# Scores of the dilated and block-sparse heads on 64 rows each, two heads side by side

## The chip, the cores and the metric

The kernel runs on one core of one Trainium2 chip. The metric is the device time of one execution in microseconds (us). Three executions of the kernel before took 2421.84, 2419.41 and 2421.93 us; their median is 2421.84.

## The reference, cut to what matters

Two transformer blocks on 512 tokens of 1024 features, all in float32. The first mixes tokens with two kinds of heads (latent attention, "MLA", and dilated windows) and has 32 routed experts; the second has softmax heads over blocks ("MoBA"), stick-breaking heads, a gated delta rule and two dense feed-forward layers. The change is in two of these places.

The dilated branch has 3 groups of 8 heads of 64 features. Group 0 looks back 128 tokens; group 1 does so within each of 4 residues of the token number modulo 4, group 2 within each of 16. Per head, tile of 128 queries and its 128 or 256 keys:

```python
s = einsum('bqhd,bkhd->bhqk', q, k) * dh ** -0.5          # 64 features are contracted
s = where(valid, s - slope[h] * delta * stride, -inf)     # a linear bias, and the window
m = max(s); p = exp(s - m); den = sum(p); o = (p / den) @ v
```

The maximum and the denominator of every group are kept, because the three groups are joined in one softmax. The MoBA heads (8, also of 64 features) come to plain causal softmax at 512 tokens: with two blocks of 256 every past block is chosen.

## The kernel before, in words

Scores need the queries and keys with the features on the partitions. Two heads of 64 features share the 128 partitions of a tile. So that one head's score can be made by a matmul over all 128 rows, the queries lie in a tile with twice the room, `dq` [128, 4 pairs, 2 heads, 512] (`mq` for MoBA): for head 0 rows 64 to 127 are zeros, for head 1 rows 0 to 63. `Dilated.q` sets these zeros with two memsets on POOL (L1724, L1725; L583, L584 for MoBA) and its `evict` writes the halves, one with ACT (L1730, L611) and one with VectorE (L1731, L612).

`Dilated.pair` does two heads of a group (four pairs a group, L1752). It works in jobs: in group 0 a job is one query tile for both heads (four jobs), in groups 1 and 2 it is two query tiles for both heads (two jobs). A job has one PSUM bank `dS` of the tag "s". In it, for each of its two or four scores: the score matmul (L1772, float32, which stands in the trace as two passes, each a weight load and a matmul) and behind it a bf16 matmul that adds bias and mask (L1775). Then VectorE takes the maxima (L1777, L1779), ACT makes one exponential per score (L1788), TensorE transposes the blocks (L1795, `dPT`), VectorE copies them (L1799, `pt`), and TensorE multiplies with the values (L1801, `dO`): 64 columns per head, head 0 to PSUM partitions 0 to 63, head 1 to 64 to 127, the two heads' products one after the other in the program.

`causal_pair` (L313 to L340) serves MLA (96 rows per head) and MoBA. For each of four query tiles and each of two heads: a bank, the score over 128 to 512 keys (L321), a bf16 mask matmul (L322), and `softmax_tile`. Then, per key tile, transposes (L330), a copy for head 0 on VectorE (L336) and for head 1 on ACT (L334), and the products with the values (L339, `OM` for MoBA).

The tag "s" has two banks, "t" two, "o" one, "acc" three. What stands in which order on an engine is not the order of the program text: a planner takes each engine's instructions as its own estimate says that their operands and buffers are ready, and among the ready ones that which stands first in the program. So products of later steps (the next group's projection `acc`, the gate products `gps`, the stick-breaking projections `sps`) stand between the steps of attention on TensorE. At run time each engine keeps that order and waits on semaphores.

Of the kernel before, what the change touches and what calls it, by code (L numbers as in the profile page):

```python
# [9 lines left out]
F32 = mybir.dt.float32  # L10
# [3 lines left out]
AF = mybir.ActivationFunctionType  # L14
# [4 lines left out]
EPS = 1e-6  # L19
# [43 lines left out]
class Model:  # L63
# [25 lines left out]
    def unit(self, src, a, b, pool=None):  # L89
        """Loads a weight unit src [128, a, b] (a * b <= 1024); returns its two float32r parts."""  # L90
# [13 lines left out]
    def split(self, hi, lo, src, eng=None):  # L104
        """hi + lo = src, each in float32r."""
# [57 lines left out]
    def feat_start(self, jobs, nk, rhs):  # L163
        """The first feature-major products after a norm: the first 256 tokens of all, then the others."""
# [7 lines left out]
    def rsqrt_mean(self, pool, ss, n, width, name):  # L172
        """(ss / n + EPS) ** -0.5 on [128, width]."""
# [7 lines left out]
    def norm_tile(self, pool, h, src, grow):  # L181
        """h = rms_norm(src) * grow."""
# [42 lines left out]
    def col(self, pool, ap, p, n, name):  # L225
        """[p, n] tile of a vector: element j * p + i at [i, j]."""
# [71 lines left out]
    def softmax_tile(self, pool, S, n, scale, bufs):  # L298
        """exp(scale * (S - max)) / sum of it, on S [128, n] in PSUM."""
# [143 lines left out]
    def vectors(self, *parts):  # L443
        """Vectors over the features as columns."""
# [12 lines left out]
    def later(self):  # L457
        """What the first products don't need: masks, vectors, what the modulation starts from."""
# [13 lines left out]
    def rows_to_col(self, pool, vec, n, name):  # L472
        """[128, n] tile of a vector of n * 128: element j * 128 + i at [i, j]."""
# [9 lines left out]
    def ada(self, n, layers=(0, 1)):  # L483
        """The next n steps of cond @ ada_w."""
# [38 lines left out]
    def ada_norm(self, pool, l, part, t, bufs=2):  # L523
        """The modulated norm of X's token tile t, transposed, to H; its second part is returned."""
# [5 lines left out]
    def add_out(self, pool, w, nk, lhs, gate, after):  # L530
        """X += gate * (lhs^T w); after(pool, t) is what follows on token tile t."""
# [13 lines left out]
    def second_mix(self):  # L545
# [9 lines left out]
        with ExitStack() as ctx:  # L555
# [12 lines left out]
            # rope tables  # L568
# [41 lines left out]
            def q_evict(sl, p):  # L610
                nc.scalar.activation(qT[:64, :, 0, sl], p[:64], AF.Copy, scale=0.125)  # L611
                nc.vector.tensor_scalar(qT[64:, :, 1, sl], p[64:], 0.125, None, op0=OP.mult)  # L612

            roped(0, q_evict)
# [47 lines left out]
            def out_part(o, r, c, t, us, tag):  # L662
                """X += gate * (o^T w_out's half r) of a token tile and half the columns."""
# [32 lines left out]
    def stick_pair(self, ap, sp, q, k, V, p, oB):  # L696
        """Two stick-breaking heads. Of key tile j, the queries from tile j on, on the free axis."""
# [100 lines left out]
    def gdn(self):  # L798
# [10 lines left out]
        with ExitStack() as ctx:  # L809
# [22 lines left out]
            # decay and step sizes, [128 tokens, tile, head]  # L832
# [55 lines left out]
            def conved(f, dst):  # L888
                """dst = silu(causal convolution of the projection's column tile f)."""
# [10 lines left out]
            def with_norms(f0, dst, extra, between=None):  # L900
                """Eight heads; returns ln of 1 / their lengths as rows, and per token."""
# [970 lines left out]
```

## Time and profile before

| | |
|---|---|
| median of three runs | 2421.84 us |
| profiled execution, first to last instruction (its own time as far as the profile shows it) | 2423.2 us |
| TensorE busy, weight loads busy | 96%, 73% of the span |
| VectorE, ACT, POOL busy | 50%, 35%, 18% |
| attention of dilated group 0, 1, 2 | about 234 to 285, 342 to 364, 444 to 475 us |
| attention of the MoBA heads | about 1060 to 1135 us |
| mean granted TensorE clock | 0.988 |

All stretches are in microseconds from the start of the span. A matmul's row in a timeline has its start and the time to its modelled end; matmuls overlap in the pipeline, so what one costs the engine is read from start to start and not from its length.

### The profile page before, as it was taken

The page shows a single profiled execution, that of the slowest core. Times are in us where ns is not written, and L with a number is a line of the kernel's source. Part 1 is how long each engine was busy: PE and PEld are TensorE (multiplying, and loading weights), DVE is VectorE, ACT ScalarE, POOL GpSimd, SP SyncE. Part 2 cuts the span into 40 slices and gives each one's busy share as a digit, 9 for nine tenths or more (in the row PEclk, how much of TensorE's full clock was granted, in tenths as well). Part 3 has the DMA queues.
Part 4 walks back from the last instruction along what each step waited for, and adds up shares of the span by engine and source line. Part 5 has one row for each costly group of instructions (what it writes and reads, how often), then busy time and mean ns, then how long its engine had stood idle before and what let it go on. Part 6 is the DMA issues. An engine that isn't in the chain of part 4 may idle for free.

```text
span 2423.2 us, 29920 instructions
## 1 busy us (share of the span) xinstructions
PE 2331.5 (96%) x11384; PEld 1761.2 (73%) x11384; DVE 1203.3 (50%) x1939; ACT 851.8 (35%) x1542; POOL 425.3 (18%) x502
## 2 busy tenths in 40 slices
PE   6989999999989999899999999999998999999998
PEld 6567899878844443676668888787667888888886
DVE  5664645455534433655347555424578466333322
ACT  5544333433211111444454223213654444322211
POOL 3233112011111110310001111111030141111111
PEclk9999999999989999999999999999999999999999
DMA  4232133445999994432115556523232123333221
GB/s 124 87 105 87 53 96 108 128 115 161 306 327 371 368 367 173 121 105 69 36 39 152 175 183 199 181 90 107 79 92 65 50 66 120 113 89 103 96 89 68
DMA packets 300281, 330.96 MB, mean 137 GB/s; under 512 B 16832, under 2 KB 241280, under 8 KB 299744
## 3 DMA queue, kind: packets, MB, share of 16 engines
q1 hardware_dynamic: 294128, 310.16, 40.9%
q0 software_dynamic: 6000, 18.79, 2.3%
q8 instruction: 92, 1.51, 0.3%
q14 instruction: 61, 0.50, 0.1%
HBM read 322.49 MB, written 6.41 MB: 136 GB/s over the span
## 4 chain that ended last, share of the span: by engine, by line
PE 83%; DVE 6%; ACT 3%; issue 3%; POOL 3%; DMA 2%; DVEq 0%; POOLq 0%; ACTq 0%
PE acc L119 8%; PE acc L120 8%; PE acc L121 8%; PE fps L119 7%; PE fps L120 7%; PE fps L121 6%; PE gps L119 3%; PE gps L121 3%; PE gps L120 3%; PE py L1453 2%; PE cps L1492 1%; PE S L321 1%; PE cps L1493 1%; PE gp L1004 1%; DMA wraw<-in_ada_w_dram 1%
## 5 line engine op out<-in xcount | busy, mean ns | idle before, releaser
L110 ACT ACTIVATE whi<-wraw 128x1024 fp32r<-128x1024 f32 (+3 forms) x295 | 300.2, 1020 | 452.4 <-PE acc L120 197.6
L114 DVE TENSOR_TENSOR wlo<-wraw,whi 128x1024 fp32r<-128x1024 f32 (+3 forms) x251 | 293.8, 1175 | 312.4 <-ACT whi L110 308.1
L120 PE MATMUL fps<-hhi,wlo 128*128 128x512 f32 (+1 forms) x768 | 286.5, 373 | 0.4 <-DVE wlo L114 0.4
L119 PE MATMUL fps<-hhi,whi 128*128 128x512 f32 (+1 forms) x768 | 286.6, 373 | 0.0
L121 PE MATMUL fps<-hlo,whi 128*128 128x512 f32 (+1 forms) x768 | 284.5, 371 | 0.7 <-DVE hlo L114 0.6
L119 PE MATMUL acc<-whi,hhi 128*128 128x512 f32 (+2 forms) x640 | 258.8, 406 | 0.5 <-DVE qx L1561 0.3
L120 PE MATMUL acc<-whi,hlo 128*128 128x512 f32 (+2 forms) x640 | 251.8, 394 | 1.3 <-DVE hlo L114 1.2
L121 PE MATMUL acc<-wlo,hhi 128*128 128x512 f32 (+2 forms) x640 | 250.8, 393 | 0.0
L114 POOL TENSOR_TENSOR wlo<-wraw,whi 128x1024 fp32r<-128x1024 f32 x44 | 108.2, 2460 | 570.4 <-ACT whi L110 555.8
L495 DVE SCALAR_TENSOR_TENSOR adaacc<-wraw,cond,adaacc 128x1024 f32<-128x1024 f32 x84 | 116.8, 1390 | 107.6 <-DMA wraw<-in_ada_w_dram 107.3
L119 PE MATMUL gps<-hhi,whi 128*128 128x512 f32 (+1 forms) x408 | 158.3, 388 | 6.5 <-DVE gy L895 4.4
L119 PEld LDWEIGHTS fps<-hhi,whi 128*128 128x128 f32 x768 | 144.4, 188 | 27.6 <-issue 0.9
L121 PEld LDWEIGHTS fps<-hlo,whi 128*128 128x128 f32 x768 | 144.3, 188 | 27.3 <-DVE hlo L114 1.1
L120 PEld LDWEIGHTS fps<-hhi,wlo 128*128 128x128 f32 x768 | 144.6, 188 | 24.9 <-DVE wlo L114 0.6
L120 PEld LDWEIGHTS acc<-whi,hlo 128*128 128x128 f32 x640 | 146.0, 228 | 16.6 <-DVE hlo L114 2.8
L121 PE MATMUL gps<-hlo,whi 128*128 128x512 f32 (+1 forms) x408 | 157.3, 387 | 0.5 <-DVE hlo L114 0.4
L119 PEld LDWEIGHTS acc<-whi,hhi 128*128 128x128 f32 x640 | 145.6, 228 | 16.5 <-issue 2.1
L120 PE MATMUL gps<-hhi,wlo 128*128 128x512 f32 (+1 forms) x408 | 156.4, 384 | 0.0
L121 PEld LDWEIGHTS acc<-wlo,hhi 128*128 128x128 f32 x640 | 145.6, 228 | 14.5 <-issue 0.8
L119 PE MATMUL acc<-whi,gh 128*128 128x512 f32 x352 | 139.1, 395 | 0.0
L120 PE MATMUL acc<-whi,gl 128*128 128x512 f32 x352 | 139.0, 395 | 0.0
L121 PE MATMUL acc<-wlo,gh 128*128 128x512 f32 x352 | 139.0, 395 | 0.0
(742 smaller groups left out, 4115.8 us busy)
## 6 DMA issues: line engine op xcount, KB each, us to landing
wraw<-in_ada_w_dram SPq DMA_DIRECT2D x96, 512.0 KB, 4.0
wraw<-in_ffn_w_in_dram SPq DMA_DIRECT2D x88, 512.0 KB, 3.9
wraw<-in_w_in_dram SPq DMA_DIRECT2D x52, 512.0 KB, 4.5
wraw<-in_ffn_w_out_dram SPq DMA_DIRECT2D x44, 512.0 KB, 3.6
eraw<-in_w_gate_dram SPq DMA_DIRECT2D x64, 256.0 KB, 7.0
eraw<-in_w_up_dram SPq DMA_DIRECT2D x64, 256.0 KB, 7.1
wraw<-in_gdn_w_in_dram SPq DMA_DIRECT2D x32, 512.0 KB, 4.3
eraw<-in_w_down_dram SPq DMA_DIRECT2D x30, 512.0 KB, 7.8
```

Of the source, the lines that this page charges most:

```text
L110: nc.scalar.activation(hi, src, AF.Copy)
L114: (eng or nc.vector).tensor_tensor(lo, src, hi.bitcast(F32), op=OP.subtract)
L119: t.matmul(out, a[0], b[0], start=start, stop=False)
L120: t.matmul(out, a[1], b[0], start=False, stop=False)
L121: t.matmul(out, a[0], b[1], start=False, stop=stop)
L321: nc.tensor.matmul(S[:, :n], qh[:, i * 128:n], kh[:, :n], start=True, stop=False)
L495: nc.vector.scalar_tensor_tensor(self.acc_ada, raw, self.cond[:, k:k + 1], self.acc_ada, op0=OP.mult, op1=OP.add)
L1004: nc.tensor.matmul(out[:, n * C:(n + 1) * C], lhsT[:, n], rhs_[:, n], start=True, stop=True)
L1453: nc.tensor.matmul(out[s], a[:, k, s], us[i][:, kk], start=start, stop=stop)
L1492: nc.tensor.matmul(ps, oh[:, t * 128:t * 128 + 128], yh[:, c], start=True, stop=False)
L1493: nc.tensor.matmul(ps, oh[:, t * 128:t * 128 + 128], yl[:, c], start=False, stop=True)
```

## The change

The queries lose the doubled room and the zeros: `dq` and `mq` are [128, 4, 512], written by one VectorE instruction per tile. A score is a matmul over the 64 rows of its head (rows 0 to 63, or 64 to 127), with 128 columns. The two heads' scores stand side by side in the program, and each head has a bank of its own, so the two banks of the tag "s" serve one step. In `pair` a step is two query tiles in group 0 and all four in groups 1 and 2, and all scores of the step come before its bias matmuls; maxima, exponentials, transposes and copies are per head; the products with the values come after both heads' copies, the heads alternating. In `causal_pair` both heads' scores of a query tile come before their two mask matmuls, for MLA too. The rest of the change is comments taken out.

```diff
 def causal_pair(self, pool, qk, V, p, O, scale, bufs):
             n = (i + 1) * 128
-            for s, (qh, kh) in enumerate(qk):
-                S = self.ps("s", name="S")
-                nc.tensor.matmul(S[:, :n], qh[:, i * 128:n], kh[:, :n], start=True, stop=False)
-                nc.tensor.matmul(S[:, n - 128:n], self.identb, self.causalb, start=False, stop=True)
-                Ps[s, i] = self.softmax_tile(pool, S, n, scale, bufs)
+            S = [self.ps("s", name="S") for _ in qk]
+            for x, (qh, kh) in zip(S, qk):
+                nc.tensor.matmul(x[:, :n], qh[:, i * 128:n], kh[:, :n], start=True, stop=False)
+            for x in S:
+                nc.tensor.matmul(x[:, n - 128:n], self.identb, self.causalb, start=False, stop=True)
+            for s, x in enumerate(S):
+                Ps[s, i] = self.softmax_tile(pool, x, n, scale, bufs)
...
  def second_mix(self):
-            qT = mp.tile([128, 4, 2, T], F32, name="mq")
+            qT = mp.tile([128, 4, T], F32, name="mq")
-            with tc.issue_after(powered):
-                nc.gpsimd.memset(qT[64:, :, 0], 0.0)
-                nc.gpsimd.memset(qT[:64, :, 1], 0.0)
-            roped(0, q_evict)
+            roped(0, lambda sl, p: nc.vector.tensor_scalar(qT[:, :, sl], p, 0.125, None, op0=OP.mult))
-                self.causal_pair(ap, [(qT[:, p, s], kT[:, p]) for s in range(2)], V, p, O, 1.0, (3, 2, 2, 5))
+                half = [slice(64 * s, 64 * s + 64) for s in range(2)]
+                self.causal_pair(ap, [(qT[h, p], kT[h, p]) for h in half], V, p, O, 1.0, (3, 2, 2, 5))
...
 def q(self, g, pool):
-        q = pool.tile([128, 4, 2, T], F32, name="dq", bufs=1)
-        with self.M.tc.issue_after(self.M.powered.ins):
-            nc.gpsimd.memset(q[64:, :, 0], 0.0)
-            nc.gpsimd.memset(q[:64, :, 1], 0.0)
+        q = self.qT[g] = pool.tile([128, 4, T], F32, name="dq", bufs=1)
         def evict(t, p):
-            nc.scalar.activation(q[:64, :, 0, sl], p[:64], AF.Copy, scale=self.gains[:64, 0, g:g + 1])
-            nc.vector.tensor_scalar(q[64:, :, 1, sl], p[64:], self.gains[64:, 0, g:g + 1], None, op0=OP.mult)
+            nc.vector.tensor_scalar(q[:, :, t * 128:t * 128 + 128], p, self.gains[:, 0, g:g + 1], None, op0=OP.mult)
...
 def pair(self, g, p):
+        wide = lambda i: 256 if g == 0 and i else 128
+        for tiles in ((0, 1), (2, 3)) if g == 0 else ((0, 1, 2, 3),):
+            at = [sum(wide(x) for x in tiles[:j]) for j in range(len(tiles))]
+            S = [M.ps("s", name="dS") for s in range(2)]
+            for j, i in enumerate(tiles):
+                more = dict(start=False, skip_group_check=True) if j else dict(start=True)
+                for s in range(2):
+                    h = slice(64 * s, 64 * s + 64)
+                    nc.tensor.matmul(S[s][:, at[j]:at[j] + wide(i)], q[h, i * 128:(i + 1) * 128],
+                                     k[h, (i + 1) * 128 - wide(i):(i + 1) * 128], stop=False, **more)
+            for s in range(2):
                 e = 2 * p + s + 2 - (2 if g else 0)
+                for j, i in enumerate(tiles):
+                    tab = self.fold if g == 2 else self.band[:, 256 - wide(i):]
+                    nc.tensor.matmul(S[s][:, at[j]:at[j] + wide(i)], self.diag[:, e], tab, start=False, stop=True,
+                                     skip_group_check=bool(j))
...
+            for s in range(2):
+                mx = dp.tile([128, 4], F32, name="dmx", bufs=3)
...
+                P = self.sp.tile([128, T], F32, name="P", bufs=5)
+                for j, i in enumerate(tiles):
+                    sl = slice(at[j], at[j] + wide(i))
+                    nc.scalar.activation(P[:, sl], S[s][:, sl], AF.Exp, bias=nm[:, j:j + 1],
+                                         accum_out=st[:, i, 8 + 2 * p + s:9 + 2 * p + s])
+                PT = M.ps("t", name="dPT")
...
+                nc.vector.tensor_copy(pt[:, :nb], PT[:, :nb])
+                pts.append(pt)
+            for z, (i, kt) in enumerate(blocks[0]):
+                for s in range(2):
+                    nc.tensor.matmul(O[64 * s:64 * s + 64, i * 128:(i + 1) * 128], V[:, kt, 2 * p + s],
+                                     pts[s][:, z * 128:(z + 1) * 128], start=kt == i - (wide(i) // 128 - 1),
+                                     stop=kt == i)
```

## Rows read from the trace of the kernel before

**Rows 1.** The page: busy time by engine, and the chain that ended last, by engine

```profile
PE 2331.5 (96%) x11384; PEld 1761.2 (73%) x11384; DVE 1203.3 (50%) x1939; ACT 851.8 (35%) x1542; POOL 425.3 (18%) x502
...
PE 83%; DVE 6%; ACT 3%; issue 3%; POOL 3%; DMA 2%; DVEq 0%; POOLq 0%; ACTq 0%
```

**Rows 2.** Stretches: length, busy us (instructions) by engine, PE clock, DMA share, GB/s

```profile
250.00:285.00 35.00, 34.76 (x230) 26.69 (x229) 20.38 (x41) 12.62 (x47) 3.84 (x13) 1.00 0.00 1
...
1060.00:1125.00 65.00, 64.88 (x300) 37.24 (x299) 48.27 (x150) 32.99 (x86) 0.60 (x1) 1.00 0.24 68
```

**Rows 3.** Tiles dS, S, dO: count, ns min/median/max, first and last start, forms

```profile
L1772 PE MATMUL dS<-dk,dq x192: 270/328/382, 234.4 to 467.5; 128*128 128x128 f32 x144, 128*128 128x256 f32 x48
...
L321 PE MATMUL S<-mk,mq x64: 271/460/697, 1061.1 to 1123.0; 128*128 128x128 f32 x16, 128*128 128x256 f32 x16, 128*128 128x384 f32 x16, 128*128 128x512 f32 x16
...
L1801 PE MATMUL dO<-pt,V x240: 272/273/476, 240.1 to 473.0; 128*64 128x128 f32 x120
```

**Rows 4.** TensorE's timeline (start, us to the last end) in group 1, 128-key scores

```profile
342.54 0.44 PE L1772 MATMUL dS<-dk,dq 128*128 128x128 f32 x2
...
342.88 0.44 PE L1772 MATMUL dS<-dk,dq 128*128 128x128 f32 x2
```

**Rows 5.** TensorE's timeline in group 0, 256-key scores

```profile
250.09 0.60 PE L1772 MATMUL dS<-dk,dq 128*128 128x256 f32 x2
250.52 0.27 PE L1775 MATMUL dS<-masks,diag 128*128 128x256 bf16 x1
250.63 0.60 PE L1772 MATMUL dS<-dk,dq 128*128 128x256 f32 x2
```

**Rows 6.** TensorE's timeline around 64-row matmuls of the delta rule

```profile
1867.54 0.40 PE L121 MATMUL gps<-hlo,whi 128*128 128x512 f32 x1
1867.77 0.40 PE L119 MATMUL gps<-hhi,whi 128*128 128x512 f32 x1
1868.10 0.68 PE L1027 MATMUL gp<-gY,gB 64*64 64x64 f32 x8
1868.70 0.55 PE L1048 MATMUL gvT<-blob,gsq 128*128 128x128 f32 x3
```

**Rows 7.** TensorE's timeline in group 2: one job's scores between another's transposes

```profile
455.35 0.27 PE L1795 MATMUL dPT<-blob,P 128*128 128x128 f32 x1
455.46 0.39 PE L1772 MATMUL dS<-dk,dq 128*128 128x128 f32 x2
455.69 0.29 PE L1795 MATMUL dPT<-blob,P 128*128 128x128 f32 x1
...
456.68 0.66 PE L1801 MATMUL dO<-pt,V 128*64 128x128 f32 x8
457.27 0.44 PE L1795 MATMUL dPT<-blob,P 128*128 128x128 f32 x2
```

**Rows 8.** ACT's timeline there: fourth and eighth of eight exponentials of two jobs

```profile
454.78 0.37 ACT L1788 ACTIVATE P<-dS,dnm 128x128 f32<-128x128 f32 x1
...
456.16 0.39 ACT L1788 ACTIVATE P<-dS,dnm 128x128 f32<-128x128 f32 x1
```

**Rows 9.** TensorE's timeline in MoBA: products with values, one head and both

```profile
1077.59 1.07 PE L339 MATMUL OM<-pt,V 128*64 128x512 f32 x2
1078.59 0.66 PE L330 MATMUL PT<-blob,P 128*128 128x128 f32 x4
...
1081.63 0.97 PE L339 MATMUL OM<-pt,V 128*64 128x384 f32 x4
1082.53 0.66 PE L330 MATMUL PT<-blob,P 128*128 128x128 f32 x4
```

**Rows 10.** Tile dq: the evictions and one of the memsets

```profile
L1730 ACT ACTIVATE dq<-dxT,dgain x12: 666/672/677, 119.8 to 407.4; 64x512 f32<-64x512 f32 x12
L1731 DVE TENSOR_SCALAR dq<-dxT,dgain x12: 756/757/758, 120.7 to 408.2; 64x512 f32<-64x512 f32 x12
L1724 POOL MEMSET dq<- x3: 1802/1803/1806, 79.6 to 323.7; 64x2048 f32 x3
```

More of the change, by code (lines that the diff above doesn't have):

```diff
@@ L608, in roped @@
                 self.proj_tok(w_in, a * 512, 512, KD, lhs, consume)
-            def q_evict(sl, p):
-                nc.scalar.activation(qT[:64, :, 0, sl], p[:64], AF.Copy, scale=0.125)
-                nc.vector.tensor_scalar(qT[64:, :, 1, sl], p[64:], 0.125, None, op0=OP.mult)
-            roped(0, q_evict)
+            roped(0, lambda sl, p: nc.vector.tensor_scalar(qT[:, :, sl], p, 0.125, None, op0=OP.mult))
             roped(1, lambda sl, p: nc.scalar.activation(kT[:, :, sl], p, AF.Copy))
@@ L1721, in q @@
         nc = self.M.nc
-        q = pool.tile([128, 4, 2, T], F32, name="dq", bufs=1)
-        with self.M.tc.issue_after(self.M.powered.ins):
-            nc.gpsimd.memset(q[64:, :, 0], 0.0)
-            nc.gpsimd.memset(q[:64, :, 1], 0.0)
-        self.qT[g] = q
+        q = self.qT[g] = pool.tile([128, 4, T], F32, name="dq", bufs=1)
         def evict(t, p):
-            sl = slice(t * 128, t * 128 + 128)
-            nc.scalar.activation(q[:64, :, 0, sl], p[:64], AF.Copy, scale=self.gains[:64, 0, g:g + 1])
-            nc.vector.tensor_scalar(q[64:, :, 1, sl], p[64:], self.gains[64:, 0, g:g + 1], None, op0=OP.mult)
+            nc.vector.tensor_scalar(q[:, :, t * 128:t * 128 + 128], p, self.gains[:, 0, g:g + 1], None, op0=OP.mult)
         self.normed(g, 0, evict)
@@ L1757, in pair @@
     def pair(self, g, p):
-        M, nc, dp, ap = self.M, self.M.nc, self.dp, self.ap
+        M, nc, dp = self.M, self.M.nc, self.dp
         q, k, V = self.qT[g][:, p], self.kT[g][:, p], self.V[g]
         O = M.ps("o", name="dO")
-        if g == 0:
-            jobs = [[(s, i) for s in range(2)] for i in range(NT)]
-        else:
-            jobs = [[(s, i) for i in (2 * b, 2 * b + 1) for s in range(2)] for b in range(2)]
-        for job in jobs:
-            S = M.ps("s", name="dS")
-            i0, nj = job[0][1], len(job)
-            n = 256 if g == 0 and i0 > 0 else 128
-            Sv = S[:, :n * nj].rearrange("p (j n) -> p j n", n=n)
-            for j, (s, i) in enumerate(job):
-                e = 2 * p + s + 2 - (2 if g else 0)
-                nc.tensor.matmul(Sv[:, j], q[:, s, i * 128:(i + 1) * 128],
-                                 k[:, (i + 1) * 128 - n:(i + 1) * 128], start=True, stop=False)
-                tab = self.fold if g == 2 else self.band[:, 256 - n:]
-                nc.tensor.matmul(Sv[:, j], self.diag[:, e], tab, start=False, stop=True)
-            mx = dp.tile([128, 4], F32, name="dmx", bufs=3)
-            nc.vector.reduce_max(mx[:, :nj], Sv, axis=AX.X)
-            nm = dp.tile([128, 4], F32, name="dnm", bufs=3)
-            nc.vector.tensor_scalar(nm[:, :nj], mx[:, :nj], -1.0, None, op0=OP.mult)
-            st = self.st[1][:, g - 1] if g else self.st[0][:, 0]
-            if g == 0:
-                nc.gpsimd.tensor_copy(st[:, i0, 2 * p:2 * p + 2], mx[:, :nj])
-            else:
-                nc.gpsimd.tensor_copy(st[:, i0:i0 + 2, 2 * p:2 * p + 2], mx.rearrange("p (a b) -> p a b", a=2))
-            P = self.sp.tile([128, T], F32, name="P", bufs=5)
-            Pv = P[:, :n * nj].rearrange("p (j n) -> p j n", n=n)
-            for j, (s, i) in enumerate(job):
-                nc.scalar.activation(Pv[:, j], Sv[:, j], AF.Exp, bias=nm[:, j:j + 1],
-                                     accum_out=st[:, i, 8 + 2 * p + s:9 + 2 * p + s])
-            PT = M.ps("t", name="dPT")
-            blocks = []
-            for j, (s, i) in enumerate(job):
-                for b in range(n // 128):
-                    z = len(blocks)
-                    nc.tensor.transpose(PT[:, z * 128:(z + 1) * 128], Pv[:, j, b * 128:(b + 1) * 128], M.ident)
-                    blocks.append((s, i, i - (n // 128 - 1) + b))
-            pt = self.sp.tile([128, T], F32, name="pt", bufs=3)
-            nb = len(blocks) * 128
-            nc.vector.tensor_copy(pt[:, :nb], PT[:, :nb])
-            for z, (s, i, kt) in sorted(enumerate(blocks), key=lambda b: (b[1][1], b[1][2], b[1][0])):
-                nc.tensor.matmul(O[64 * s:64 * s + 64, i * 128:(i + 1) * 128], V[:, kt, 2 * p + s],
-                                 pt[:, z * 128:(z + 1) * 128], start=kt == max(0, i - n // 128 + 1), stop=kt == i)
@@ new lines, in pair @@
+        st = self.st[1][:, g - 1] if g else self.st[0][:, 0]
+        wide = lambda i: 256 if g == 0 and i else 128
[9 more added lines that the diff above has]
+            for s in range(2):
+                e = 2 * p + s + 2 - (2 if g else 0)
+                for j, i in enumerate(tiles):
+                    tab = self.fold if g == 2 else self.band[:, 256 - wide(i):]
+                    nc.tensor.matmul(S[s][:, at[j]:at[j] + wide(i)], self.diag[:, e], tab, start=False, stop=True,
+                                     skip_group_check=bool(j))
+            n = len(tiles)
+            blocks, pts = [[], []], []
+            for s in range(2):
+                mx = dp.tile([128, 4], F32, name="dmx", bufs=3)
+                if wide(tiles[0]) == wide(tiles[-1]):
+                    w = wide(tiles[0])
+                    nc.vector.reduce_max(mx[:, :n], S[s][:, :n * w].rearrange("p (j n) -> p j n", n=w), axis=AX.X)
+                else:
+                    for j, i in enumerate(tiles):
+                        nc.vector.reduce_max(mx[:, j:j + 1], S[s][:, at[j]:at[j] + wide(i)], axis=AX.X)
+                nm = dp.tile([128, 4], F32, name="dnm", bufs=3)
+                nc.vector.tensor_scalar(nm[:, :n], mx[:, :n], -1.0, None, op0=OP.mult)
+                nc.gpsimd.tensor_copy(st[:, tiles[0]:tiles[0] + n, 2 * p + s], mx[:, :n])
+                P = self.sp.tile([128, T], F32, name="P", bufs=5)
+                for j, i in enumerate(tiles):
+                    sl = slice(at[j], at[j] + wide(i))
+                    nc.scalar.activation(P[:, sl], S[s][:, sl], AF.Exp, bias=nm[:, j:j + 1],
+                                         accum_out=st[:, i, 8 + 2 * p + s:9 + 2 * p + s])
+                PT = M.ps("t", name="dPT")
+                for j, i in enumerate(tiles):
+                    for b in range(wide(i) // 128):
+                        z = len(blocks[s])
+                        nc.tensor.transpose(PT[:, z * 128:(z + 1) * 128], P[:, z * 128:(z + 1) * 128], M.ident)
+                        blocks[s].append((i, i - (wide(i) // 128 - 1) + b))
+                pt = self.sp.tile([128, T], F32, name="pt", bufs=3)
+                nb = len(blocks[s]) * 128
+                nc.vector.tensor_copy(pt[:, :nb], PT[:, :nb])
[5 more added lines that the diff above has]
+                                     stop=kt == i)
```

## The prediction, made before the changed kernel was built or run

> **What bounds the kernel now.** Read first the page's busy times and its chain [rows 1]: TensorE is busy 96% of the span and is 83% of the chain that ended last. Then the stretches in which attention runs [rows 2]: TensorE is busy 34.8 of 35 us in group 0 and 64.9 of 65 in MoBA, at a granted clock of 1.00 (2.4 GHz), while VectorE has 58% and 74% and the DMA engines little. Nothing sets the pace there but TensorE's queue, and what fills it beside attention is products of later steps, of which there are always more. So I price the change in TensorE's time alone: a microsecond more or less there moves everything behind it. The third view is the timeline of TensorE, for what one instruction costs and for what stands between the scores.
>
> **Scores now.** There are 96 dilated scores of two passes (192 rows), 72 of 128 keys and 24 of 256, and 32 MoBA scores, 8 of each width [rows 3]. A 256-key score takes 0.43 us until its bias matmul starts, and 0.11 more until the next score [rows 5]. A 128-key score with its bias repeats after 0.34 [rows 4], so the score is 0.23. In proportion to the 256-key row, 384 and 512 keys are 0.65 and 0.86. Group 0 has 8 x 0.23 + 24 x 0.43 = 12.2 us, groups 1 and 2 have 64 x 0.23 = 14.7, MoBA 8 x (0.23 + 0.43 + 0.65 + 0.86) = 17.4: 44.3 us of scores. If two heads always ran side by side, half would go, 22 us.
>
> **That two halves of the array can run at once.** No row shows 64 rows by 128 columns. The nearest is the products with the values, two heads on 64 columns each: four blocks, eight passes, start to next instruction 0.59 us [rows 7], against 1.00 us for two passes of one head over 512 columns, which is as much streaming as four blocks of 128 of one head [rows 9]. So two heads nearly share their time. I take full sharing for scores that are neighbours in the queue, and none for scores that are not; the ends are none at all and a half.
>
> **What a change of mode costs.** The delta rule has matmuls on 64 rows by 64 columns. The product before them follows its predecessor by 0.23 us and they follow it by 0.33; out of them, eight passes at 0.68 of modelled length, the next full matmul comes 0.60 after the first start [rows 6]. Entering costs 0.10. The way out I take as the same, 0.10 (ends: 0, if this gap is only the last pass's own, and 0.2, if also a weight load that was hidden is bared). An excursion into 64-row mode and back is 0.2 us, ends 0.1 to 0.3. The Trainium skill has a rule on this ("TensorEngine Tiling (Array Packing)", Key Properties): a change of tiling mode, not of the tile within one, drains the engine. It gives no price, and it speaks against this change, since the bias matmuls and the transposes stay on all 128 rows. The row agrees for a mode that halves rows and columns; no run here shows halved rows alone. By the rule all 69 excursions below count; if only halved columns drained, the sum would be 13.8 us lower, 2427.
>
> **Which scores will be neighbours.** This decides. The planner takes what is ready, earliest in the program first. The tag "s" has two banks, and a step now needs one for each head. In the first step of a group both are free: scores of both heads are ready together. Afterwards head 0's bank comes free when its exponentials are done and head 1's four exponentials later, which is 1.38 us [rows 8]. In that time TensorE has four scores of head 0 ready (0.92 us), and head 1's are not. The trace shows what happens to ready work of low place: one job's scores stand singly between the other job's transposes as these come, one score, one transpose, repeated [rows 7]. Today that costs nothing, for all are in one mode; then each single score is an excursion. The same holds in MoBA, where a score waits for its own bank and the heads alternate.
>
> **The sum for scores.** Gains: the first pair of groups 1 and 2, 8 x 0.23 / 2 each, and the first step of group 0, (2 x 0.23 + 2 x 0.43) / 2, together 2.5 us. Of the other 44.3 - 5.0 = 39.3 us I take one in four to be side by side by accident (ends: none, all), 39.3 / 4 / 2 = 4.9. Losses: groups 1 and 2, two first pairs with one excursion and six with four (three for head 0, which is split as in [rows 7], one for head 1), 26; group 0, eight steps, one excursion for the first and two for each other, 15; MoBA, 16 query tiles, two each, less 4 for the one in four, 28. That is 69 x 0.2 = 13.8. Net +6.4 us.
>
> **Products with the values.** Today a job's probabilities of both heads come in one copy, so all its blocks are ready at once and the heads alternate: 0.59 us for eight passes. After the change each head has its own transposes and copy, the second at least its 1.38 us of exponentials later [rows 8]. The program still lists the heads alternately, but head 0's blocks are ready alone, and they stand before everything else that is ready. MoBA shows this today: there the heads' copies are separate, and at the widest tile two passes of one head stand alone, 1.00 us, with transposes behind them; the four passes of two heads at 384 columns, three quarters of the width but both heads, take 0.90 [rows 9]. For one head four blocks cost 1.00, three 0.79 by proportion and 0.15 of fixed cost. Groups 1 and 2: two runs per pair at 1.00 instead of 0.59, 8 pairs, +6.6 us. Group 0 per pair: 2 x (0.79 + 1.00) = 3.58 instead of three runs of 0.59 and one of two blocks, about 0.37, 2.14: +1.44, four pairs, +5.8. Together +12.4 (ends: 0, if TensorE is so far behind that both copies are there, and 12.4).
>
> **Costed at nothing.** Bias matmuls stand in a row instead of between scores: 0.11 each today [rows 5]; as their streaming is half of that, up to 96 x 0.055 = 5 us may go; I take none. The q evictions lose 12 ACT instructions of 0.67 us, VectorE's stay as many on twice the partitions at 0.76 [rows 10]; ACT is at 35% and hides it, and if it did not, 8 us at most would be gained. The POOL memsets, about 3.6 us for each of four q tiles, go; POOL is at 18% [rows 1], and at most one of them could have held up a norm: 0 to 4 us. Group 0 has two more maxima per pair on VectorE, at 58% there. Head 1's score is a new wait: what is queued behind it on TensorE is filler that the planner believed late; it costs where the chip's exponentials come later than planned, 0 to 0.5 us for 30 steps, 15 us at the far end. In MLA the order of two scores and two masks only delays head 0's maximum when both banks are free, 0 to 0.9 us in 16 tiles; the projections cover it.
>
> **Forecast.** 2423.2 + 6.4 + 12.4 = 2442.0 us for the profiled execution, which stands 1.4 above the median of the runs shown; so 2441.
>
> **The rivals.**
>
> *Pairs hold (faster).* The place is TensorE's queue at each step's scores: if the planner gets to them only when both banks are free, all pair. The price: -22 us, with one excursion for each of 8 + 8 + 16 steps, +6.4: -15.7, so 2406, or 2401 with the bias row. It decides from the point at which three in four of the scores are neighbours and the heads' products stay paired. For it: between attention's bursts TensorE is backlogged, and in group 2 both jobs' scores fall into one burst. Against it: the single scores between transposes [rows 7], whose order comes from the same planner.
>
> *Scores pair, values split.* -15.7 + 12.4 = -3.3: 2419, no change that can be told. For it: the products depend on copies that are at least 1.4 us apart, the scores on banks that may be close.
>
> *Nothing is shared.* 64-row scores of float32 do not overlap at all. Then the 7.4 us of shared gain in the forecast are missing, and excursions are the same: 2448. For it: no row has two row halves at work; the delta rule's 64-row passes [rows 6] are all of one half. Against it: the column halves do share.
>
> *A rule of its own.* The Trainium skill ("TensorE: Matmul & The Clock Gate", Measured speedup vs the span model) gives 3.07 times for four row tiles of 512 columns, so 77% of full sharing; by that, as an estimate, two heads' scores would save 44.3 - 44.3 / 1.54 = 15.5 us where I have 22 at full pairing, and the faster rival would end at 2413. Its chance lies within that rival's.
>
> *The chain leads.* Both banks bound up in one step mean that head 0 of the next step cannot run ahead of head 1. If that leaves TensorE waiting 1 us in each of the 30 later steps, it is 30 us on top of half the losses: 2461.
>
> **How the numbers follow.** Two runs of this kernel can be told apart from about 0.2%, 4.8 us. Forecast or nothing shared (2430 to 2456), 0.62, slower. The chain leads, 0.05, slower. Pairs hold (2401 to 2414), 0.19, faster. Scores pair and values split (2412 to 2426), 0.14: two parts in three of it within 0.2%, one part faster. That makes faster 0.24, same 0.09, slower 0.67. The likeliest case's own range is 2430 to 2456: excursions at 0.1 to 0.3 (-7 to +7), bias row (-5), accident pairing of none to a half (+5 to -5). As cases of both signs hold much of the chance, the range given reaches to the middle of the faster one: 2409 to 2456.
>
> **What would show it.** In the profile after, `dS` matmuls are 64*128. Right, if TensorE's timeline has them mostly in runs of one head, with a gap of 0.1 us on either side, if `dO` comes in runs of eight passes that last 1.0 us and not 0.6, and if the stretch from the first `dS` of group 0 to the last `dO` of group 2, and that of MoBA, are longer by 10 to 15 and by 3 to 6 us. Wrong, if scores of two heads start within 0.01 us of each other throughout, if `dO` keeps 0.59 for its eight passes, or if the difference appears in stretches that the change doesn't touch.

## The result, and the profile after

The changed kernel takes 2447.47 us, the median of four runs (2444.11 to 2448.72), beside 2421.89 for the kernel before in the same runs: ratio 1.0103, 95% interval [1.0091, 1.0116]. It is 1.0% slower, 6 us above the forecast of 2441 and inside its range. The profiled execution spans 2446.9 us.

The page after, busy time and the chain, to be read beside [rows 1]: nothing here tells the two kernels apart. TensorE is at 96% of the span and 83% of the chain in both; its busy time has grown by 19 us and the span by 24.

```profile
PE 2350.4 (96%) x11384; PEld 1766.3 (72%) x11384; DVE 1197.4 (49%) x1947; ACT 842.6 (34%) x1526; POOL 411.8 (17%) x494
...
PE 83%; DVE 6%; POOL 3%; ACT 3%; issue 3%; DMA 2%; POOLq 0%; DVEq 0%; ACTq 0%
```

The tiles after, which answer to [rows 3] (count, ns min/median/max, first and last start, forms):

```profile
L1761 PE MATMUL dS<-dk,dq x192: 271/323/481, 241.5 to 488.4; 64*128 64x128 f32 x144, 64*128 64x256 f32 x48
L1799 PE MATMUL dO<-pt,V x240: 272/273/325, 248.0 to 495.9; 128*64 128x128 f32 x120
L321 PE MATMUL S<-mk,mq x64: 271/482/694, 1081.0 to 1148.3; 64*128 64x128 f32 x16, 64*128 64x256 f32 x16, 64*128 64x384 f32 x16, 64*128 64x512 f32 x16
L341 PE MATMUL OM<-pt,V x64: 272/459/644, 1099.3 to 1161.4; 128*64 128x512 f32 x16, 128*64 128x384 f32 x16, 128*64 128x256 f32 x16, 128*64 128x128 f32 x16
```

The starts are the reading. The first dilated score comes at 241.5 us, not 234.4: 7.1 us are gone before the dilated heads begin. That place moves by itself: in x3 and x10 below, whose TensorE program is that of before up to there, it is 233.8 and 231.3, so the 7.1 holds to some 3 us. From it to the last product it is 254.4 us instead of 238.6 (+15.8). From the first MoBA score to the last `OM` ([rows 9] are of that stretch) it is 80.4 instead of 73.9 (1061.1 to 1135.0; +6.5). This last length is no measure of cost: other products stand in the stretch too, and it is 79.7 to 80.7 us in every run below with MoBA on 64 rows, also in those that are faster than the kernel before.

**The dilated heads.** TensorE's timeline in group 1, a first step and a step of the next pair of heads:

```profile
356.37 1.16 PE L1761 MATMUL dS<-dk,dq 64*128 64x128 f32 x8
357.46 0.40 PE L1767 MATMUL dS<-masks,diag 128*128 128x128 bf16 x4
...
358.44 1.16 PE L1761 MATMUL dS<-dk,dq 64*128 64x128 f32 x8
...
362.64 0.33 PE L1791 MATMUL dPT<-blob,P 128*128 128x128 f32 x1
362.89 0.48 PE L1761 MATMUL dS<-dk,dq 64*128 64x128 f32 x2
363.31 0.33 PE L1791 MATMUL dPT<-blob,P 128*128 128x128 f32 x1
...
364.24 0.43 PE L1799 MATMUL dO<-pt,V 128*64 128x128 f32 x2
364.61 0.33 PE L1791 MATMUL dPT<-blob,P 128*128 128x128 f32 x1
364.86 0.93 PE L1761 MATMUL dS<-dk,dq 64*128 64x128 f32 x8
365.73 1.09 PE L1799 MATMUL dO<-pt,V 128*64 128x128 f32 x14
366.74 0.49 PE L1761 MATMUL dS<-dk,dq 64*128 64x128 f32 x2
```

Four readings. From one transpose to the next with one score between them it is 0.67 us, where [rows 7] have 0.34. The first step is not side by side: it is four scores of one head (four biases behind them, products, then the other head's four), and four scores in 1.09 us share nothing. Six later runs of four scores share in part: eight passes take 0.87 us (364.86 to 365.73). And the products with the values are not two runs of eight passes at 1.0 us: fourteen passes take 1.01 (365.73 to 366.74), with two passes ahead of them (0.37 us, 364.24 to 364.61).

**MLA.** The stretch from 180 us to where the first dilated score stood before, after and (second fence) before; the columns are as in [rows 2]:

```profile
180.00:234.40 54.40, 49.13 (x229) 33.77 (x229) 22.87 (x49) 17.29 (x36) 12.89 (x18) 0.97 0.20 58
```

```profile
180.00:234.40 54.40, 54.40 (x261) 39.21 (x260) 25.00 (x51) 20.65 (x41) 17.21 (x20) 1.00 0.20 58
```

TensorE was never idle there and now is for 5.3 us. Its granted clock, the last column but two, is 0.97 instead of 1.00. What it waits for, in the kernel after (waits of TensorE, 180 to 242 us), and then VectorE's and POOL's timelines at that place, with the idle time ahead of an instruction and its releaser in brackets:

```profile
PE OA L341 <- DVE pt L338: 4.1, 1, 4.1
PE S L321 <- ACT P L307: 1.1, 1, 1.1
```

```profile
200.13 0.69 DVE L1705 TENSOR_TENSOR dx<-acc,dr 128x512 f32<-128x512 f32 x1 [4.52 <-POOL dr L178]
...
200.81 0.67 DVE L338 COPY pt<-PT 128x512 f32<-128x512 f32 x1
```

```profile
192.36 5.71 POOL L1685 TENSOR_SCALAR diag<-blob 128x128 bf16<-128x128 f32 x10 [4.61 <-PE S L323]
198.15 0.20 POOL L177 TENSOR_SCALAR dm<-dss 128x8 f32<-128x8 f32 x1
198.43 1.67 POOL L178 TENSOR_TENSOR dr<-dm,mhalf 128x8 f32<-128x8 f32 x1
```

It is a queue behind a wait, over three engines. The ten fills of the bias diagonals (5.7 us on POOL) stand ahead of the root `dr` of the dilated norm; VectorE's product `dx` waits for `dr`; the copy `pt`, for which TensorE waits, stands behind `dx`. Before, with the heads one after the other, all copies `pt` of this place were done by 200.2 us, and POOL began the next `dr` at 201.9 us, so the `dx` that waited for it stood behind them (VectorE and, last, POOL, before):

```profile
199.94 0.29 DVE L336 COPY pt<-PT 128x128 f32<-128x128 f32 x1 [1.22 <-PE PT L330]
203.61 0.69 DVE L1709 TENSOR_TENSOR dx<-acc,dr 128x512 f32<-128x512 f32 x1 [1.42 <-POOL dr L178]
201.91 1.67 POOL L178 TENSOR_TENSOR dr<-dm,mhalf 128x8 f32<-128x8 f32 x1
```

The wait costs more than its length. TensorE's wait of 4.1 us ends at 201.5, and just behind it, from 202.7 to 206.1, the granted clock is 0.50 (1.2 GHz, the lower of its two levels; columns as in [rows 2]):

```profile
202.70:206.10 3.40, 3.40 (x8) 1.25 (x7) 0.87 (x2) 0.60 (x1) 0.00 (x0) 0.50 0.52 152
```

By our estimate 3.4 us at half the clock lose 1.7 us; with the 5.3 us of idle time that is 7.0, near the 7.1.

### The profile page after: what moved, and what is told of

The parts are those of the page before. It is cut to its first block, busy times and chain, and to the rows that moved or that the text cites. A ratio compares the mean times of both kernels' runs of the same rounds, so it can differ in the third digit from the quotient of the medians.

```text
span 2446.9 us, 29898 instructions
## 1 busy us (share of the span) xinstructions
PE 2350.4 (96%) x11384; PEld 1766.3 (72%) x11384; DVE 1197.4 (49%) x1947; ACT 842.6 (34%) x1526; POOL 411.8 (17%) x494
## 4 chain that ended last, share of the span: by engine, by line
PE 83%; DVE 6%; POOL 3%; ACT 3%; issue 3%; DMA 2%; POOLq 0%; DVEq 0%; ACTq 0%
PE acc L119 8%; PE acc L121 8%; PE acc L120 8%; PE fps L120 6%; PE fps L119 6%; PE fps L121 6%; PE gps L119 3%; PE gps L121 3%; PE gps L120 3%; PE py L1449 2%; PE S L321 1%; PE cps L1488 1%; PE dS L1761 1%; PE cps L1489 1%; PE gp L1000 1%
```

## The experiments

Five timed rounds each; brackets hold the 95% interval of the ratio. A difference in us is the ratio less 1, times 2423.

**x1 and x2: MLA's order alone, and the change without it.**

```diff
+ if scale != 1.0:      # x1: MLA only, the new order; x2 the other way round
      S, S; mask, mask; softmax, softmax
+ else:
+     S, mask, softmax; S, mask, softmax
```

> The kernel before, and of the change only the new order in MLA: both heads' scores, then both masks, then both softmaxes. Dilated and MoBA heads as before. Theory A (the order in MLA is what moved the first dilated score from 234.4 to 241.5 us): 5 to 9 us slower than before, ratio 1.002 to 1.004, and TensorE waits on the exponentials or the copies somewhere between 180 and 234 us. Theory B, the prediction's own step (the order costs nothing there, the projections cover it; the shift has another cause, such as another order of all that stands around it because the dilated part of the program is another): within 1.5 us of before, and the first dilated score at 234 to 236 us.

Measured 2429.63 us, ratio 1.0028 [1.0017, 1.0038]; first dilated score at 240.7; the same two waits of 4.1 and 1.2 us, and around the end of the first 6.8 us (198.4 to 205.2) at a granted clock of 0.50. Theory A.

> The changed kernel, with MLA put back to the order of before (score, mask, softmax of one head and then of the other). Theory A (MLA's order costs what it seems to and adds to the rest): 6 to 8 us faster than the changed kernel, 2439 to 2442, so 17 to 20 us slower than before, ratio 1.007 to 1.008; first dilated score at 234 to 236 us. Theory B (the time lost in MLA is given back or lost again later anyway): within 2 us of the changed kernel, 2445 to 2449.

Measured 2436.65 us, 1.0058 [1.0044, 1.0071]; first dilated score at 232.0, and no wait of TensorE from 180 to 242 us. It is 0.45% or 11 us faster than the changed kernel, more than the 6 to 8 expected, but the two intervals leave some 4 us either way: MLA's order costs 7 to 11 us.

**x11 and x12: is it that queue?** The fills move to ACT, in the changed kernel and in the one before.

```diff
- nc.gpsimd.tensor_scalar(self.diag[:, e], M.ident, 2.0 ** (1 - e), None, op0=OP.mult)
+ nc.scalar.activation(self.diag[:, e], M.ident, AF.Copy, scale=2.0 ** (1 - e))
```

> The changed kernel, MLA's new order kept; only the ten fills of the bias diagonals move from POOL to ACT. In the changed kernel POOL's 5.7 us of fills stand ahead of the norm's root (dr), VectorE's product with it (dx) waits 4.52 us for that, and behind dx on VectorE stands the copy pt for which TensorE waits 4.12 us. Theory A (this queue is what MLA's new order costs): the waits of 4.1 us at 197 us are gone or under 1 us, and the kernel is 3.5 to 6 us faster than the changed one, 2441 to 2444, ratio to before 1.008 to 1.009. Theory B (the products pt and the exponentials are late by themselves, both heads in lockstep, and the queue only carries it): TensorE still waits 3 us or more for pt there and the time stays within 1.5 us of the changed kernel.

> The control to x11_fills_act: the kernel before, with the ten fills on ACT too. Theory A (before, POOL's fills held up nothing that TensorE waits for): within 1.5 us of before. Theory B (fills on POOL cost in any order, by queueing or otherwise): 2 us or more faster.

x11: 2441.93 us, 1.0075 [1.0062, 1.0089], 0.28% or 7 us below the changed kernel, a little over theory A's 3.5 to 6. x12: 2423.37, 0.9999 [0.9990, 1.0008], theory A. VectorE's order is unchanged, only its wait is shorter (1.53 us for `dr`), and TensorE's waits are:

```profile
PE OA L341 <- DVE pt L338: 1.1, 1, 1.1
PE S L321 <- ACT P L307: 1.1, 1, 1.1
```

So POOL's fills were most of what MLA's new order cost, and cost nothing in the old one. About 2 us of waits are left. The 1.1 us for `pt` still come by the same queue: `PT` was done by 198 us, and the copy stood behind `dx` until 199.8. The 1.1 us for exponentials were not followed further.

**x3: the price of an excursion.** The kernel before, MoBA's queries unpadded; each score has a mask or another full-array product behind it. The fills of zeros and four of the evictions go with the padding.

```diff
- qT = [128, 4, 2, T], zeros in the other head's rows
+ qT = [128, 4, T];  scores from qT[64 * s:64 * s + 64, p], kT[64 * s:64 * s + 64, p]
```

> The kernel before, with only the MoBA queries unpadded: its 32 scores run on 64 rows each, in the old order, so a mask matmul on 128 rows stands behind every score and no two scores of two heads can run side by side. This measures the price of an excursion into 64-row mode alone. Theory A (the prediction's step: entering and leaving cost 0.2 us together, ends 0.1 to 0.3): 32 x 0.2 = 6.4 us slower than before, 3 to 10. Theory B (halved rows do not drain the array; only halved columns would): within 1.5 us of before. Theory C (a score on half the rows is also quicker or slower in itself): the pitch from a score to its mask differs from the 0.43 us of 256 keys by more than 0.1 us.

Measured 2427.07 us, 1.0018 [1.0009, 1.0027]: 4 us slower, theory A. TensorE's timeline, and (second fence) the same widths before:

```profile
1086.10 1.12 PE L321 MATMUL S<-mk,mq 64*128 64x512 f32 x2
1087.15 0.23 PE L322 MATMUL S<-masks,identb 128*128 128x128 bf16 x1
...
1089.50 0.49 PE L321 MATMUL S<-mk,mq 64*128 64x128 f32 x2
1089.92 0.23 PE L322 MATMUL S<-masks,identb 128*128 128x128 bf16 x1
```

```profile
1061.08 0.38 PE L321 MATMUL S<-mk,mq 128*128 128x128 f32 x2
1061.30 0.22 PE L322 MATMUL S<-masks,identb 128*128 128x128 bf16 x1
...
1087.26 1.02 PE L321 MATMUL S<-mk,mq 128*128 128x512 f32 x2
1088.11 0.22 PE L322 MATMUL S<-masks,identb 128*128 128x128 bf16 x1
```

From the start of a score to what follows it is now 0.42, 0.63, 0.84 and 1.05 us for the four widths; the shortest before were 0.22, 0.43, 0.64 and 0.86. So 0.2 us are added whatever the width, the estimate of the prediction; theory C's sign, a pitch off by more than 0.1 us, is there too, but a cost that does not grow with the width is not one of streaming. Halved rows alone thus pay for the change. That agrees with the rule that the prediction weighed (the Trainium skill, "TensorEngine Tiling (Array Packing)", Key Properties: a change of tiling mode drains the engine); the trace shows the gap and not what fills it. Over the 32 scores the trace has 4.0 us of it and not 6.4, because before many stood above their shortest (512 keys: 0.86 to 0.96) and that went; the masks take 1.1 us more.

**x4: the new order without the 64 rows.** As x2, with the padded queries of before, so that TensorE's order is that of x2.

> The changed kernel with MLA's old order, and with the zero-padded queries of before: scores on 128 rows, all else (a bank per head, program order, copies per head) as in the changed kernel. Beside x2_mla_back it shows what the 64 rows alone do, beside the kernel before what the new order alone does. Theory A (the prediction's terms: rows cost 6.4 us net, split products cost the rest): 4 to 9 us faster than x2_mla_back, 2431 to 2437, so 10 to 14 us slower than before. Theory B (the products with the values turned out to stay paired, so the new order costs little, 3 to 5 us, and the rows cost the rest): 2425 to 2428, 12 us or more faster than x2_mla_back. Theory C (the rows gain by sharing, and the order costs all): slower than x2_mla_back.

Measured 2427.86 us, 1.0022 [1.0013, 1.0031]. The time is theory B's, the distance to x2 theory A's: the order costs 5 us, the rows with all that goes with the padding 9 (x2 less x4). Of the order, x4's trace has 2.8 us more in `dO` than before and 2.8 us more of waits between 230 and 500 us, and 2.5 us less in `dS` with its biases, which now stand in a row. The same place in both, x4 first:

```profile
348.71 0.27 PE L1809 MATMUL dPT<-blob,P 128*128 128x128 f32 x1
348.82 0.39 PE L1779 MATMUL dS<-dk,dq 128*128 128x128 f32 x2
349.04 0.27 PE L1809 MATMUL dPT<-blob,P 128*128 128x128 f32 x1
```

```profile
352.95 0.33 PE L1798 MATMUL dPT<-blob,P 128*128 128x128 f32 x1
353.21 0.49 PE L1768 MATMUL dS<-dk,dq 64*128 64x128 f32 x2
353.63 0.33 PE L1798 MATMUL dPT<-blob,P 128*128 128x128 f32 x1
```

A transpose and a score repeat after 0.33 us and after 0.68. The score takes 0.2 more, and the transpose behind it another 0.15 (0.26 to the next instruction instead of 0.11). Summed over the trace, start to next start, the rows add 6.4 us to `dS` and its biases, 4.4 to `dPT` and 2.0 to `S` and its masks, 13 in all; the 9 on the clock have some 4 us either way.

**x5 to x7: make the pairs hold.** x5 is x2 with a step's scores queued behind the last transpose of the step before (`issue_after` holds instructions back in the planner's order until another has been placed). x6 is x5 with MoBA as before. x7 is x5 with MoBA's masks first and both heads' scores behind the second mask.

```diff
+ with issue_after(last transpose of the step before):          # x5
      for i in tiles: for s in (0, 1): score(s, i)
+ mask(0), mask(1); with issue_after(mask(1)): score(0), score(1)   # x7, MoBA
```

> As x2_mla_back (MLA in its old order), and in the dilated heads the scores of a step are queued behind the last transpose of the step before, so that both heads' banks are free when the first score is taken; MoBA as in the changed kernel. The planner then lists the scores of both heads next to each other, where before they stood singly between transposes. Theory A (neighbours on two row halves share their time, the rival 'pairs hold'): 36 lone scores at 0.2 us and a slower transpose behind each go, about 10 us, and of 27 us of dilated scores up to half, less 0.4 us for each of 12 steps: 2417 to 2425, 12 to 20 us faster than x2_mla_back; passes of the two heads start within 0.01 us of each other. Theory B (a 128-key pass is set by its weight load of 0.11 us, and the loads follow each other whichever half they fill, so nothing is shared): only the lone scores go, 2426 to 2431, and eight passes start 0.11 us apart. Theory C (the wait costs more than it brings, since TensorE has no other work in the queue there): 2435 or more, with idle time of TensorE before the scores.

> x5_pairs with the MoBA heads as in the kernel before (padded queries, score and mask of one head after the other). Theory A (MoBA's part of the change costs on its own about what x3_moba_rows and the MoBA stretches say): 3 to 6 us faster than x5_pairs, and the MoBA stretch from first score to last product again 73 to 75 us. Theory B (the sharing of its 512-key pairs already pays for the excursions there): within 2 us of x5_pairs.

> x5_pairs, and in MoBA the masks of both heads come first in their banks and the scores of both heads, each cut into its last 128 keys and the rest, behind them, so that these too are neighbours. Theory A (sharing): MoBA's 17.4 us of scores become half and 0.2 us for each of 16 query tiles, 12 us: 4 to 7 us faster than x6_pairs_moba_old and the fastest of the four or near it, 2410 to 2418. Theory B (pairs start a weight load or more apart, so they share little; MoBA's 512-key pairs took 1.40 us to the mask in x2_mla_back, where full sharing would be 1.05): within 2 us of x6_pairs_moba_old.

Measured 2434.55 (1.0054 [1.0040, 1.0067]), 2433.36 (1.0046 [1.0032, 1.0059]) and 2427.79 (1.0022 [1.0013, 1.0031]). x5 misses theory A by 10 us and is nearest to theory C in time, though its idle time stands before transposes and not before scores; against x2 it gains nothing beyond the noise. x6 is 2 us below x5: theory B, but A's 3 us are within the noise, and its MoBA stretch is the 73.8 us that A named. x7's 6 us below x6 are theory A's, from a higher start. In x5 the pairs do hold but for the first steps: starts of the two heads' passes are 0.01 us apart, as theory A said. `dS` with its biases loses 9.7 us and `dPT` 4.1 against x2 (start to next start, idle time left out); but TensorE now waits (waits of TensorE, 230 to 500 us, and one place):

```profile
PE dPT L1803 <- ACT P L1797: 5.5, 4, 2.0
```

```profile
291.41 0.93 PE L1803 MATMUL dPT<-blob,P 128*128 128x128 f32 x3 [1.99 <-ACT P L1797]
```

Three of the four waits for exponentials stand between 260 and 292 us, in group 0, and the fourth at the end of group 1: with both banks bound up in one step, no score of the next step runs ahead under the exponentials. That is the mechanism of the rival "the chain leads", at 6 us and not 30. The clock takes a part too: in x5 it is granted at 0.50 from 284.8 to 288.2 and from 291.6 to 295.0, around the waits of 1.3 and 2.0 us there, and in x7's trace, with the same waits, from 283.5 to 297.2; in x2's and before it stays at 1.00 in group 0.

**x8: biases first.** As x7, but the dilated biases too open the banks, and the scores stand behind the last bias.

> x7_pairs_all, but in the dilated heads the biases come first in the banks and the scores behind the last of them; nothing is held back behind transposes any more, and the biases can fill time between transposes. Theory A (what matters is only that the scores are neighbours): within 2 us of x7_pairs_all. Theory B (holding scores behind the last transpose made each step's chain longer, or the biases in a mode of their own now save excursions): 2 to 6 us faster than x7_pairs_all. Theory C (the biases now break the transposes' order or wait for the second bank with other work behind them): slower by 2 us or more.

Measured 2422.19 us, 0.9997 [0.9988, 1.0006]; 6 us faster than x7 (theory B in time), as fast as the kernel before. How much of the 6 us is the order's own is open: the waits are much the same, and x8's trace has 3.4 us at half the clock in group 0 where x7's has 13.7. Now first steps are pairs as well:

```profile
350.31 1.16 PE L1778 MATMUL dS<-dk,dq 64*128 64x128 f32 x16
351.40 0.63 PE L119 MATMUL acc<-whi,hhi 128*128 128x512 f32 x1
```

Eight scores of two heads take the 1.09 us that four of one head take in the kernel after. Sharing is complete here: less the 0.2 us of the excursion, 0.89 us for what is 8 x 0.22 = 1.76 one by one. (The estimate from the Trainium skill's 3.07 for four tiles, "TensorE: Matmul & The Clock Gate", Measured speedup vs the span model, was 77%; this row has more, 81% even with the excursion left in.) What is left against it are 5.0 us of waits for exponentials, mostly in group 0 again, and 3 us in `dO`.

**x9 and x10: versions put together.** x9: MLA and group 0 as before; groups 1 and 2 with biases first and paired scores, but exponentials, transposes, copies and products as before; MoBA as in x7. x10: the kernel before with x7's MoBA alone.

> A version put together from what the runs so far show. MLA and dilated group 0 as in the kernel before (padded queries, a bank per query tile); groups 1 and 2 with a bank per head, biases first, the scores of both heads behind the last bias, but from the exponentials on as before (both heads' tiles in turn, one copy for two query tiles of both heads); MoBA with masks first and paired scores. Theory A (each term adds: the 64-row dilated scores of groups 1 and 2 and of MoBA share their time, group 0 keeps its short chain, and the products with the values run four blocks of both heads together again): the waits of 5 us of x8_bias_first in group 0 and 2 to 3 us of products go, so 2412 to 2418, ratio 0.996 to 0.998. Theory B (the chain of groups 1 and 2, with both banks bound up in one step, now makes TensorE wait there instead): 2420 to 2426, with idle time before the transposes of groups 1 and 2.

> The kernel before, with only MoBA on 64 rows, masks first and both heads' scores behind the second mask. Theory A (scores side by side save half of 17.4 us and pay 16 excursions of 0.2 us): 3 to 6 us faster than before, ratio 0.9975 to 0.999, and 7 to 10 us faster than x3_moba_rows. Theory B (the second head's bank comes late and TensorE waits or delays the softmax): within 2 us of before.

Measured 2415.38 us, 0.9966 [0.9952, 0.9979], and 2416.91, 0.9972 [0.9962, 0.9983]. Both beat both kernels. x9 is theory A; x10 is theory A's direction, and its 7 us below before and 11 below x3 are a little more than A's 3 to 6 and 7 to 10. The intervals of the two overlap, so that groups 1 and 2 gain anything on the clock isn't shown; in x9's trace `dS` with biases is 6.7 us shorter than before and 2.3 us of waits for exponentials have come. Its products run eight passes as before:

```profile
348.61 0.66 PE L1835 MATMUL dO<-pt,V 128*64 128x128 f32 x8
349.19 0.94 PE L1789 MATMUL dS<-dk,dq 64*128 64x128 f32 x12
```

MoBA is the clear case: the same 64 rows cost 4 us with scores alone (x3) and gain 7 with scores in pairs (x10). In x10 two scores of 512 keys, cut into 128 and 384, take 1.07 us to the next product, where one alone takes 1.05 in x3:

```profile
1066.79 0.49 PE L325 MATMUL S<-mk,mq 64*128 64x128 f32 x4
1067.12 0.81 PE L328 MATMUL S<-mk,mq 64*128 64x384 f32 x4
1067.86 0.44 PE L343 MATMUL PT<-blob,P 128*128 128x128 f32 x2
```

## Why the prediction came out as it did

The direction was right, and so was the place but for MLA. The time is 6 us off, but that nearness is in part luck: the sum got there by errors that offset each other.

| part | forecast, us | measured, us | from |
|---|---|---|---|
| 64 rows (scores, transposes) | +6.4 | +9 | x2 less x4 |
| new order, products with the values | +12.4 | +5 | x4 less before |
| MLA's order | 0 | +7 to +11 | x1; after less x2 |
| sum | +18.8 | +25 | after less before |

Each measured part has 2 to 5 us either way, and the rows' 9 holds what the fills and evictions gave back, which the prediction took at nothing.

- **The mode change** was sized right at 0.2 us for a lone score (x3). The term came out larger for two reasons: the 41 excursions counted for the dilated heads were 56 runs of 64-row scores in the trace (36 of one score, 10 of two, 10 of four), and a transpose behind one loses another 0.15 us. That way in and way out cost 0.10 each is in the trace: in the eight passes at 356.37 the second starts 0.21 us behind the first and what follows 0.21 behind the last, and those between follow after 0.11.
- **The neighbours** were right in kind: lone scores between transposes, head 0's as its bank comes free. Wrong were the first steps, taken as side by side (2.5 us): head 0's four scores went out alone. In MoBA 5 of 16 query tiles were side by side, near the one in four assumed (27 runs of 64-row scores, 28 counted).
- **Sharing** was assumed complete, and x8 and x10 show that it can be; "nothing is shared" is out, and that its 2448 is the time measured is a coincidence. But neighbours of the changed kernel shared less: of MoBA's five, the one of 256 keys took 0.64 us to what follows, that of 384 keys 1.29 and the three of 512 keys 1.40, where full sharing would be 0.63, 0.84 and 1.05.
- **The products with the values** are the step that failed in size. "Head 0's blocks are ready alone, and they stand before everything else" did not come: in every step of the trace head 0's first block goes alone (two passes) and all others follow in one run of ten or fourteen, as the program lists them, head by head in turn. Our reading is that the planner keeps this order because all of them write one bank; no run tests that. x4, with padded queries, has the same runs, so it is not the rows' doing. It costs 2.8 us in all instead of 12.4.
- **Biases in a row** were costed at nothing, with 5 us at most; x4 has 2.5 us less there.
- **MLA's order** is the step that failed in kind. "Only delays head 0's maximum ... the projections cover it" looked at TensorE alone. What was queued on VectorE behind another wait, and on POOL ahead of that, was not looked at. That the granted clock would fall at such a wait is in no part of the prediction.
- **The two stretches** grew by 15.8 and 6.5 us, each just above what was named (10 to 15, 3 to 6), but the second would have been a poor sign either way, as x10 shows. The 7.1 us ahead of the first dilated score lie where the prediction had costed the change at nothing.
- **"Pairs hold"** was priced at 2406 for all heads. Forced, it gives 2422 (x8): the shared scores are there, 13 us less in the trace with biases and masks, but the waits for exponentials, mostly in group 0, take 5 us back, the products 3, and the granted clock its part. In MoBA, where x10 waits 2.2 us in all, it pays.
- **The range's** lower end, 2409, is called the middle of 2401 to 2414; that is 2407.5. Nothing rests on it.

## What to carry to other kernels

Here half-array scores paid only where they stood next to each other, and a lone one cost 0.2 us and a transpose late by 0.15. What put them there: open the accumulators with the full-array operand (mask or bias) of both heads and queue the half-array ones behind the last of them. Then look whether the longer step makes TensorE wait. An edit that changes when an engine's copies become ready is to be followed on every in-order queue that it enters, and one engine further: ten fills on an engine that is 17% busy cost 7 us.

## What was not expected of the hardware

- A lone 64-row float32 score cost 0.2 us more at 128 keys and at 512 alike, so the price is not one of streaming; the full transpose behind it started its next instruction after 0.26 us instead of 0.11.
- Passes of one head on 64 rows with 128 keys follow each other after 0.11 us, as on 128 rows; passes of two heads on two halves start together (256 keys in x2: four passes, mask after 0.63 us, as after one lone score of x3).

```profile
1074.53 0.70 PE L322 MATMUL S<-mk,mq 64*128 64x256 f32 x4
1075.16 0.28 PE L324 MATMUL S<-masks,identb 128*128 128x128 bf16 x2
```

- Neighbours of 512 keys in the same kernel took 1.40 us to the mask, not 1.05; the second head's first pass starts 0.34 us behind the first's. In x10, behind their 128-key parts, the 384-key parts start together; which part of that order did it was not separated.
- The granted clock was 0.50 for 3.4 to 13.7 us next to waits of TensorE of 1 to 4 us (after, x1, x5, x7, x8 above). No run holds the waits and lets the clock alone, and x11's trace has 6.8 us of it in group 0 (275.4 to 282.3) behind a wait of only 0.6 us, so how the two hang together is not shown.
